# Two transformer blocks on one core: four products that take the high and the low part of their input side by side

## The chip, the core and the metric

The kernel runs on one core of one Trainium2 chip as a single launch. The metric is the device time of a launch in microseconds (us). Before the change three runs gave 1110.01, 1111.19 and 1111.45 us; their median is 1111.19 us. The engines are called PE (matrix products), PEld (loading the stationary operand of a product), DVE (vector engine), ACT (scalar engine), POOL and SP. Each engine works through its own list of instructions in the order in which the program issues them, and waits for others by semaphores.

## What is computed

Two transformer blocks over 256 tokens of width 1024, in float32. The products that the change touches lie in the first block:

```
u = rms_norm(h, norm_mix)
z, xbc, dt_raw, q_a, c_kv, k_rope, gate_ssd, gate_mla = split_cols(u @ w_in, ...)
xbc = silu(causal_depthwise_conv(xbc, conv_w, conv_b))      # 4 taps along the tokens
xs, bm, cm = split_cols(xbc, (2048, 512, 512))
...                                                         # state space scan, 4 groups of 8 heads
y = y * silu(z)
...
q = rms_norm(h, norm_xattn) @ w_xq                          # attention over 256 memory rows
k, v = split(rms_norm(mem, norm_mem) @ w_xkv)
```

The four outputs that are made in another way are x (2048 columns of `w_in`), z (2048), the memory keys k (1024) and the cross queries q (1024). The B and C columns of `w_in`, the gates and the memory values stay as they are, and so do the experts of the first block and all of the second block.

## The kernel before, in words

**Precision.** An operand a is kept as a high part ah, its value rounded to the type that PE multiplies at full speed (fp32r), and a low part al = a - ah. A product is ah·bh + ah·bl + al·bh, three matmuls that add up in one PSUM tile (`mm3`, L263 to L265). The input u has its two parts in the tiles `uh` and `ul` (128 partitions, 8 blocks of 128 features, 256 tokens).

**Weights.** They come in units of 128x1024 numbers. A transfer on SP's queue fills `raw`; ACT rounds it to `whi` (L237); DVE makes `wlo = raw - whi` (L238). `run` issues these splits up to three units (`LP`) ahead of the unit that PE multiplies, and each ring of tiles (`raw`, `whi`, `wlo`) has four places, so a split also waits until PE is done with the unit four back.

**The products with features on partitions** (`gemm_fm`). A unit holds 4 of the 8 feature blocks for two chunks of 128 output columns. An item is one chunk with one unit: 4 feature blocks, 12 matmuls of 128x128 weights against 256 tokens. Two units, four items, give a pair of chunks, each in the first 256 columns of a PSUM tile of 512 (`acc`, 4 buffers). After a chunk's last matmul its evacuation is issued at once, in the same item:

- x (`ev_x`, `conv`): ACT applies the first tap and the bias to the PSUM tile (L704), then DVE adds three more taps, each reading the PSUM tile again (L707).
- z (`ev_z`, L777), memory keys (`ev_k`, L1122) and cross queries (`ev_q`, L1182): one copy by ACT.

**Order.** `schedule` merges three lists (closing steps, the chain of small steps, the large products) by fixed costs and by latencies in a table; `run` issues the items in that order, with the splits of later units between them. The large products of this stage run as: B and C mixed with z of groups 0 and 1; x of group 0 (from about 78 us); x of group 1 mixed with half of a gate product (91 to 119 us); z of group 2; x of group 2 (138 to 149 us); z and x of group 3 mixed; the other gates. The small steps of a group g, in their order: silu of x and z (`sil`), the product C·B (`cb`, L797 on PE), transposes of x scaled by dt (`xt`, L785, L787), eight decay matrices (`decay`: PE L809 to L813, ACT's exponentials L816, DVE's product M, L817), and four products with them (`ymm`, PE L828, DVE L834 and L836). The decays take turns with the products: four decays, product 0, two decays, product 1, two decays, products 2 and 3. `bcs` is the silu of all of B and C (`bT`, `cT`), after which the first `cb` can run.

The lines that decide how the evacuation of x works before the change:

```
nc.scalar.activation(y, src, AF.Identity, bias=..., scale=...)               # src: the PSUM tile
for j in (2, 1, 0):
    o = 3 - j
    nc.vector.scalar_tensor_tensor(y[:, o:], src[:, :T - o], c[...], y[:, o:], op0=ALU.mult, op1=ALU.add)
```

Of the kernel before, what the change touches and what calls it, by code (L numbers as in the profile page):

```python
# [9 lines left out]
F32 = mybir.dt.float32  # L10
F32R = mybir.dt.float32r
# [7 lines left out]
P = 128  # L19
NT = 2  # L20
T = 256
# [91 lines left out]
class K:  # L113
# [147 lines left out]
    def mm3(self, out, ah, al, bh, bl, start, stop):  # L261
# [2 lines left out]
        mm(out, ah, bl, start=False, stop=False)  # L264
        mm(out, al, bh, start=False, stop=stop)  # L265

    def acc(self):
        return self.pp.tile([P, 512], F32, tag="acc", name=self.nm("acc"), bufs=4)

# [83 lines left out]
            out += a[i:i + n] + b[i:i + n]  # L353
        return out

    def gemm_fm(self, w, c0, nch, kt, xT, evac, name, deps=(), held=None):


        items = []
        hiT, loT = xT  # L360
        for i in range(0, nch, 2):
            st = {}
            for k0 in range(0, kt, 4):
                nk = min(4, kt - k0)
                u = self.unit(w, k0, nk, c0 + i * P, 256)
                for c in range(2):
                    def fn(u=u, k0=k0, c=c, st=st, i=i, nk=nk):
                        if k0 == 0:
                            st[c] = self.chb() if held is not None and i == 4 else self.acc()
                        a = st[c][:, :T]  # L370
                        for kk in range(nk):
                            k = k0 + kk
                            s = slice(c * P, (c + 1) * P)
                            self.mm3(a, u.hi[:, kk, s], u.lo[:, kk, s], hiT[:, k, :], loT[:, k, :],
                                     start=(k == 0), stop=(k == kt - 1))
                        if k0 + 4 >= kt and (held is None or i >= 6):
                            evac(i + c, a)
                    if k0 + 4 >= kt and held is not None and i < 6:
                        held.append(Item(lambda c=c, i=i, st=st: evac(i + c, st[c][:, :T]), name=f"{name}.{i + c}"))
                    items.append(Item(fn, [u], nk * 3 * 0.109, f"{name}.{i + c}" if k0 + 4 >= kt and (held is None or i >= 6) else None))  # L380
        self.set_deps(items, deps)
        return items
# [100 lines left out]
    def phase_a(self):  # L483
# [43 lines left out]
            nc.gpsimd.tensor_copy(self.identb, self.ident)  # L527
            nc.gpsimd.tensor_copy(nmb, self.c[:, C_NEGM:C_NEGM + P])

        uh = pu.tile([P, 8, T], F32R, name="uh", tag="uh")  # L530
        ul = pu.tile([P, 8, T], F32R, name="ul", tag="ul")
        A["u"] = u = (uh, ul)
        chain, main = [], []

        def start_a():
# [162 lines left out]
                  Item(lambda: qnorm(1), cost=1.1, name="qn")]  # L698


        def conv(src, ch, y):

            c = self.cols
            nc.scalar.activation(y, src, AF.Identity, bias=c[:, 96 + ch:97 + ch], scale=c[:, 72 + ch:73 + ch])  # L704
            for j in (2, 1, 0):
                o = 3 - j
                nc.vector.scalar_tensor_tensor(y[:, o:], src[:, :T - o], c[:, 24 * j + ch:24 * j + ch + 1], y[:, o:],  # L707
                                               op0=ALU.mult, op1=ALU.add)
# [47 lines left out]
    def ssd_group(self, g):  # L756
# [9 lines left out]
        def ev_x(i, a):  # L766
            if i == 0:
                st["xT"] = ps.tile([P, 4, T], F32, name=self.nm("xT"), tag="xT", bufs=3)
            A["conv"](a, 4 * g + i, st["xT"][:, i, :])
        xdep = [("cols", 0)] + ([(f"g{g - 3}.fin", 0)] if g >= 3 else [])  # L770
        xg = self.gemm_fm(w_in, 2048 + 512 * g, 4, 8, A["u"], ev_x, f"x{g}", xdep)

        def ev_z(i, a):
            if "zs" not in A:
                A["zs"] = self.sp.tile([P, 2, 4, T], F32, name="zs", tag="big8")
            st["z"] = A["zs"][:, g % 2]
            nc.scalar.copy(st["z"][:, i, :], a)  # L777
        zg = self.gemm_fm(w_in, 512 * g, 4, 8, A["u"], ev_z, f"z{g}", [(f"g{g - 2}.y3", 0)] if g >= 2 else [])
        ch = []

        def xt(t):
# [294 lines left out]
    def tail(self):  # L1076
# [24 lines left out]
        def mem_c(t):  # L1101
            def fn():
                if t == 0:
                    A["m"] = tuple(self.cols8(i).bitcast(F32R) for i in (self.S_MH, self.S_ML))
                self.norm_c(("m", t), *A["m"], t, D)
            return fn

# [11 lines left out]
        def ev_k(c, a):  # L1119
            if c == 0:  # L1120
                A["kx"] = self.cols8(self.S_KX)
            nc.scalar.copy(A["kx"][:, c, :], a)  # L1122

        def ev_v(t, b, a):
            if t == 0 and b == 0:
# [4 lines left out]
        fill += self.gemm_fm(w, 0, 8, 8, self.lazy("m"), ev_k, "kx", [("m1", 2)])  # L1130
        fill += self.gemm_tm(w, 1024, 1024, 2, 8, self.lazy("m"), ev_v, "vx")


# [45 lines left out]
        def ev_q(c, a):  # L1179
            if c == 0:  # L1180
                st["q"], st["xp"] = self.cols8(self.S_MH), self.cols8(self.S_ML)
            nc.scalar.copy(st["q"][:, c, :], a)  # L1182
        qx = self.gemm_fm(I["w_xq"][0], 0, 8, 8, self.lazy("u"), ev_q, "qx", [("nx1", 2), ("vx.1", 0)])
        sc = 1.0 / 16

        def scores(hh, t):
# [1031 lines left out]
        return self.schedule([start, hg, sb, nrm, main])  # L2218


class _Lazy:

    def __init__(self, d, key, i=None):
# [32 lines left out]
```

## Time and profile before

| | |
|---|---|
| median of three runs | 1111.19 us |
| the profiled execution | 1112.61 us, of which its span is 1110.8 us |
| PE busy | 1049.5 us (94%) |
| PEld busy | 895.8 us (81%) |
| DVE busy | 632.7 us (57%) |
| ACT busy | 515.0 us (46%) |
| POOL busy | 142.6 us (13%) |
| mean granted clock of PE | 0.983 of full speed |

The share of busy time is a mean over stages with different limits. PE's matmuls overlap in the record (a matmul is shown for 0.28 us though the next one starts 0.12 us later), so a busy PE is not a PE without gaps; what a matmul costs in a stream is read from the distance between starts.

### The profile page before, as it was taken

Reading aid. Unit: us, or ns where it says so; the run is one execution under the profiler, and the core shown is the slowest. Engines: PE = TensorE matmul, PEld = TensorE weight load, DVE = VectorE, ACT = ScalarE, POOL = GpSimd, SP = SyncE. Lnnn points to the kernel's source line nnn. Section 1 sums busy time; section 2 is a strip of 40 time slices with the busy share of each in tenths; the row PEclk is TensorE's granted clock in tenths of the full one; section 3 lists DMA queues with packets and bytes.
Section 4 is the critical chain, followed back from the end, with each engine's and each line's share of the span. In section 5 each row is a group of like instructions: output and inputs, shape, how many; then the busy total and the mean of one; then the engine's idle time right before and its main releaser. Section 6 shows DMA issues by size and latency. Waiting matters only on the chain. (4 is left out here: it accounts for less than half of the span.)

```text
span 1110.8 us, 18654 instructions
## 1 busy us (share of the span) xinstructions
PE 1049.5 (94%) x7433; PEld 895.8 (81%) x7433; DVE 632.7 (57%) x1070; ACT 515.0 (46%) x900; POOL 142.6 (13%) x187
## 2 busy tenths in 40 slices
PE   6999999999999899999998897997999999999998
PEld 6999888878887698987675553697888799999876
DVE  4887788766766654545211110278865665555445
ACT  4658676645554454532000000166577555454433
POOL 5410221230002100001000000153501100000000
PEclk9999999999999999999999998998999999999999
DMA  7665434464443999569999999853523465556642
GB/s 255 188 191 153 132 115 139 135 181 137 135 144 115 311 348 314 161 219 327 420 413 420 413 418 413 312 177 104 189 73 120 132 219 180 190 174 192 188 149 95
DMA packets 135035, 241.33 MB, mean 217 GB/s; under 512 B 6924, under 2 KB 88336, under 8 KB 127776
## 3 DMA queue, kind: packets, MB, share of 16 engines
q1 hardware_dynamic: 132160, 231.31, 60.6%
q0 software_dynamic: 2496, 7.74, 2.2%
q8 instruction: 60, 0.98, 0.4%
q10 hardware_dynamic: 288, 1.05, 0.3%
q14 instruction: 31, 0.25, 0.1%
HBM read 239.02 MB, written 1.05 MB: 216 GB/s over the span
## 5 line engine op out<-in xcount | busy, mean ns | idle before, releaser
L238 DVE TENSOR_TENSOR wlo<-raw,whi 128x1024 fp32r<-128x1024 f32 (+1 forms) x240 | 293.5, 1235 | 156.8 <-ACT whi L237 156.1
L237 ACT CAST whi<-raw 128x1024 fp32r<-128x1024 f32 (+1 forms) x240 | 247.3, 1042 | 122.5 <-PE acc L265 59.3
L263 PE MATMUL acc<-ew,whi 128*128 128x256 f32 x528 | 150.2, 284 | 1.3 <-ACT whi L237 0.9
L265 PE MATMUL acc<-ew,wlo 128*128 128x256 f32 x528 | 149.8, 284 | 1.5 <-DVE wlo L238 1.5
L264 PE MATMUL acc<-ew,whi 128*128 128x256 f32 x528 | 149.8, 284 | 0.1
L263 PE MATMUL acc<-uh,whi 128*128 128x256 f32 x384 | 111.2, 290 | 0.0
L264 PE MATMUL acc<-ul,whi 128*128 128x256 f32 x384 | 108.6, 283 | 0.0
L265 PE MATMUL acc<-uh,wlo 128*128 128x256 f32 x384 | 108.5, 283 | 0.0
L263 PEld LDWEIGHTS acc<-ew,whi 128*128 128x128 f32 x528 | 100.5, 190 | 2.0 <-ACT whi L237 1.3
L265 PEld LDWEIGHTS acc<-ew,wlo 128*128 128x128 f32 x528 | 100.2, 190 | 2.1 <-DVE wlo L238 2.1
L264 PEld LDWEIGHTS acc<-ew,whi 128*128 128x128 f32 x528 | 100.3, 190 | 0.6 <-DVE ew L1753 0.6
L263 PEld LDWEIGHTS acc<-uh,whi 128*128 128x128 f32 x384 | 73.5, 191 | 0.8 <-issue 0.3
L264 PEld LDWEIGHTS acc<-ul,whi 128*128 128x128 f32 x384 | 73.6, 192 | 0.2
L265 PEld LDWEIGHTS acc<-uh,wlo 128*128 128x128 f32 x384 | 73.5, 191 | 0.0
L1556 PE MATMUL acc<-ew,xe 128*32 128x256 f32 x688 | 59.1, 406 | 9.0 <-DMA ew<-in_w_exp_gate_dram 5.1
L263 PE MATMUL acc<-whi,uh 128*128 128x512 f32 (+1 forms) x160 | 62.6, 391 | 0.5 <-ACT whi L237 0.5
L1515 PEld LDWEIGHTS acc<-Gr,h 128*128 128x128 f32 x256 | 54.5, 299 | 10.6 <-issue 9.6
L264 PE MATMUL acc<-wlo,uh 128*128 128x512 f32 (+1 forms) x160 | 61.3, 383 | 1.8 <-DVE wlo L238 1.8
L265 PE MATMUL acc<-whi,ul 128*128 128x512 f32 (+1 forms) x160 | 61.0, 381 | 0.4 <-DVE ul L422 0.4
L1515 PE MATMUL acc<-Gr,h 128*128 128x128 f32 x256 | 54.6, 373 | 5.8 <-DVE Gr L1496 5.8
L1556 PEld LDWEIGHTS acc<-ew,xe 128*32 128x32 f32 x688 | 35.0, 116 | 27.8 <-DMA ew<-in_w_exp_gate_dram 6.5
L263 PE MATMUL acc<-whi,ew 128*128 128x512 f32 x112 | 45.2, 404 | 1.2 <-ACT ew L421 1.2
(558 smaller groups left out, 2173.1 us busy)
## 6 DMA issues: line engine op xcount, KB each, us to landing
raw<-in_w_in_dram SPq DMA_DIRECT2D x84, 512.0 KB, 4.3
ew<-in_w_exp_down_dram SPq DMA_DIRECT2D x23, 1024.0 KB, 17.0
raw<-in_w_gate_up_dram SPq DMA_DIRECT2D x44, 512.0 KB, 3.8
ew<-in_w_exp_gate_dram SPq DMA_DIRECT2D x17, 1024.0 KB, 16.2
ew<-in_w_exp_up_dram SPq DMA_DIRECT2D x16, 1024.0 KB, 16.6
raw<-in_w_down_dram SPq DMA_DIRECT2D x22, 512.0 KB, 4.2
raw<-in_w_ssd_out_dram SPq DMA_DIRECT2D x16, 512.0 KB, 4.6
raw<-in_w_xkv_dram SPq DMA_DIRECT2D x16, 512.0 KB, 6.3
```

The source lines that it names most:

```text
L237: self.nc.scalar.copy(hi[:, :m], u.raw[:, :m])
L238: self.nc.vector.tensor_sub(lo[:, :m], u.raw[:, :m], hi[:, :m].bitcast(F32))
L263: mm(out, ah, bh, start=start, stop=False)
L264: mm(out, ah, bl, start=False, stop=False)
L265: mm(out, al, bh, start=False, stop=stop)
L1515: nc.tensor.matmul(p[:, j * P:(j + 1) * P], x, st["Gr"][:, t, :], start=(part is None and t == 0), stop=(t == 1 and (part is None or j == 3)))
L1556: nc.tensor.matmul(a[j][CAP * i:CAP * i + CAP, :256], xe[:, k, i * CAP:i * CAP + CAP], w, start=(k == 0), stop=(k == 7))
```

## The change

The two parts of u become one tile `u` with the parts side by side, `[P, 8, 2, T]`; the class `Parts` gives the high part, the low part, or both as one operand of 512 columns. The memory rows get the same layout in the two tiles that they had. For x, z, memory keys and cross queries `mm_wide` takes the place of `mm3`: one matmul of the weights' high part against both parts (512 columns, filling the whole PSUM tile), and one of the weights' low part against the high part (256 columns, added to the first half). The chunk then stands in two halves that must be added: `halves` copies the second half to SBUF with ACT and adds the first half with DVE. For x the sum goes to a new SBUF tile `cx` (2 buffers), and the four taps read that tile.

```diff
+    def mm_wide(self, out, ah, al, b, k, last):
+        mm = self.nc.tensor.matmul
+        bw = b.both(k)
+
+        def wide():
+            mm(out, ah, bw, start=(k == 0), stop=(k == last))
+
+        def narrow():
+            mm(out[:, :T], al, b.hi[:, k, :], start=False, stop=False)
+        for f in (narrow, wide) if k == last else (wide, narrow):
+            f()
+
+    def halves(self, out, a):
+        self.nc.scalar.copy(out, a[:, T:])
+        self.nc.vector.tensor_add(out, a[:, :T], out)
...
-                        a = st[c][:, :T]
+                        a = st[c][:, :T] if wide is None else st[c]
...
+                            if wide is not None:
+                                self.mm_wide(a, u.hi[:, kk, s], u.lo[:, kk, s], wide(), k, kt - 1)
+                                continue
...
-        uh = pu.tile([P, 8, T], F32R, name="uh", tag="uh")
-        ul = pu.tile([P, 8, T], F32R, name="ul", tag="ul")
-        A["u"] = u = (uh, ul)
+        A["uw"] = Parts([pu.tile([P, 8, 2, T], F32R, name="u", tag="u")])
+        A["u"] = u = uh, ul = A["uw"].hi, A["uw"].lo
...
-        def conv(src, ch, y):
+        def conv(src, ch, y, wide=False):
             c = self.cols
+            if wide:
+                x = ps.tile([P, T], F32, name=self.nm("cx"), tag="cx", bufs=2)
+                self.halves(x, src)
+                src = x
             nc.scalar.activation(y, src, AF.Identity, bias=c[:, 96 + ch:97 + ch], scale=c[:, 72 + ch:73 + ch])
...
-            A["conv"](a, 4 * g + i, st["xT"][:, i, :])
+            A["conv"](a, 4 * g + i, st["xT"][:, i, :], True)
...
-            nc.scalar.copy(st["z"][:, i, :], a)
+            self.halves(st["z"][:, i, :], a)
...
-            nc.scalar.copy(A["kx"][:, c, :], a)
+            self.halves(A["kx"][:, c, :], a)
...
-            nc.scalar.copy(st["q"][:, c, :], a)
+            self.halves(st["q"][:, c, :], a)
```

The order of the items does not change, since their costs and latencies do not. In the whole program PE issues 384 matmuls fewer, DVE 48 additions more and ACT 16 copies more (for z, keys and queries the copy was there before). At two places this is what stands on an engine.

ACT, at the first pair of chunks of x in group 1 (`acc` are the two chunks' PSUM tiles, `xT` the result, `cb` the next small step, `whi` a unit's split), before:

```order
L237 CAST whi_1209<-raw_1046 128x1024 [waits DMAHW5_49,PE_49]
L704 ACTIVATE xT_1227<-acc_1181,cols 128x256 [waits PE_49]
L704 ACTIVATE xT_1227<-acc_1194,cols 128x256 [waits PE_49]
L800 COPY cb_1251<-ch_1248 128x384 [waits PE_49]
L237 CAST whi_1253<-raw_1085 128x1024 [waits DMAHW6_49]
L816 ACT_TABLE_LOAD
```

and now:

```order
L237 CAST whi_1124<-raw_981 128x1024 [waits DMAHW5_49,PE_49]
L282 COPY cx_1139<-acc_1104 128x256 [waits PE_49]
L729 ACTIVATE xT_1138<-cx_1139,cols 128x256 [waits DVE_49]
L282 COPY cx_1154<-acc_1113 128x256 [waits PE_49]
L729 ACTIVATE xT_1138<-cx_1154,cols 128x256 [waits DVE_49]
L826 COPY cb_1164<-ch_1161 128x384 [waits PE_49]
L237 CAST whi_1166<-raw_1018 128x1024 [waits DMAHW6_49]
L842 ACT_TABLE_LOAD
```

Between the copy of a chunk and its first tap ACT now waits for DVE, and the second chunk's copy, the next split and the decays' exponentials stand behind that wait.

DVE, at the same pair, before:

```order
L238 TENSOR_TENSOR wlo_1210<-raw_1046,whi_1209 128x1024 [waits DMAHW5_49,PE_49,Activation_49]
L707 SCALAR_TENSOR_TENSOR xT_1227<-acc_1181,cols,xT_1227 128x255 [waits Activation_49]
L707 SCALAR_TENSOR_TENSOR xT_1227<-acc_1181,cols,xT_1227 128x254 [waits DVE_49]
L707 SCALAR_TENSOR_TENSOR xT_1227<-acc_1181,cols,xT_1227 128x253 [waits DVE_49]
L707 SCALAR_TENSOR_TENSOR xT_1227<-acc_1194,cols,xT_1227 128x255 [waits Activation_49]
```

and now:

```order
L238 TENSOR_TENSOR wlo_1125<-raw_981,whi_1124 128x1024 [waits DMAHW5_49,PE_49,Activation_49]
L283 TENSOR_TENSOR cx_1139<-acc_1104,cx_1139 128x256 [waits Activation_49]
L732 SCALAR_TENSOR_TENSOR xT_1138<-cx_1139,cols,xT_1138 128x255 [waits Activation_49]
L732 SCALAR_TENSOR_TENSOR xT_1138<-cx_1139,cols,xT_1138 128x254 [waits DVE_49]
L732 SCALAR_TENSOR_TENSOR xT_1138<-cx_1139,cols,xT_1138 128x253 [waits DVE_49]
L283 TENSOR_TENSOR cx_1154<-acc_1113,cx_1154 128x256 [waits Activation_49]
L732 SCALAR_TENSOR_TENSOR xT_1138<-cx_1154,cols,xT_1138 128x255 [waits Activation_49]
```

Each chunk has one addition more on DVE, and after it the next instruction of DVE waits for ACT, which itself waited for that addition.

## Rows read from the trace of the kernel before

**Rows 1.** Busy times by window: us, engines (x instructions), PEclk, DMA share, GB/s

```profile
100.00:125.00 25.00, 23.92 (x181) 19.74 (x180) 22.66 (x37) 20.09 (x42) 4.08 (x6) 1.00 0.52 160
...
225.00:250.00 25.00, 22.97 (x132) 19.31 (x129) 16.00 (x27) 11.15 (x23) 10.48 (x13) 0.93 0.59 175
```

**Rows 2.** Timeline of PE in two streams: start us, duration us, then the instruction

```profile
95.95 0.28 PE L263 MATMUL acc<-uh,whi 128*128 128x256 f32 x1
...
96.91 0.28 PE L265 MATMUL acc<-uh,wlo 128*128 128x256 f32 x1
...
226.81 0.39 PE L263 MATMUL acc<-whi,uh 128*128 128x512 f32 x1
...
227.95 0.39 PE L265 MATMUL acc<-whi,ul 128*128 128x512 f32 x1
```

**Rows 3.** Groups by shape: count, busy us, mean ns, idle before and its releasers

```profile
L777 ACT COPY zs<-acc 128x256 f32<-128x256 f32 x16 | 5.9, 381 | 9.1 <-PE acc L265 9.0
...
L1223 DVE TENSOR_TENSOR ul<-ch,uh 128x256 fp32r<-128x256 f32 x8 | 3.4, 425 | 3.0 <-ACT uh L1222 3.0
...
L704 ACT ACTIVATE xT<-acc,cols 128x256 f32<-128x256 f32 x16 | 9.0, 575 | 5.8 <-PE acc L265 5.7
...
L707 DVE SCALAR_TENSOR_TENSOR xT<-acc,cols,xT 128x254 f32<-128x254 f32 x16 | 7.7, 482 | 0.6
...
L435 DVE SCALAR_TENSOR_TENSOR qy<-sm,rpow,grow 128x256 f32<-128x256 f32 x2 | 1.0, 478 | 0.0
```

**Rows 4.** Timeline of DVE, groups 0 and 1: in brackets idle before, its releaser

```profile
88.47 1.23 DVE L238 TENSOR_TENSOR wlo<-raw,whi 128x1024 fp32r<-128x1024 f32 x1 [0.55 <-ACT whi L237]
89.61 2.94 DVE L707 SCALAR_TENSOR_TENSOR xT<-acc,cols,xT 128x255 f32<-128x255 f32 x6
...
103.38 1.22 DVE L238 TENSOR_TENSOR wlo<-raw,whi 128x1024 fp32r<-128x1024 f32 x1
...
114.73 1.22 DVE L238 TENSOR_TENSOR wlo<-raw,whi 128x1024 fp32r<-128x1024 f32 x1
...
120.47 1.78 DVE L817 TENSOR_TENSOR M<-M,cb 128x384 f32<-128x384 f32 x2 [0.33 <-ACT M L816]
```

**Rows 5.** Timeline of ACT, 90 to 100 us

```profile
90.39 0.57 ACT L704 ACTIVATE xT<-acc,cols 128x256 f32<-128x256 f32 x1 [0.87 <-PE acc L265]
...
94.53 1.04 ACT L719 ACTIVATE cT<-cT 128x1024 f32<-128x1024 f32 x1
...
99.26 1.01 ACT L704 ACTIVATE xT<-acc,cols 128x256 f32<-128x256 f32 x2
```

**Rows 6.** Timeline of PE, 97 to 123 us

```profile
97.03 0.59 PE L797 MATMUL ch<-cT,bT 128*128 128x256 f32 x2
...
108.49 0.28 PE L265 MATMUL acc<-uh,wlo 128*128 128x256 f32 x1
...
121.40 0.62 PE L828 MATMUL ch<-M,xd 128*64 128x256 f32 x2 [0.79 <-DVE M L817]
122.30 0.86 PE L828 MATMUL ch<-M,xd 128*64 128x256 f32 x6 [0.29 <-DVE M L817]
```

**Rows 7.** Timeline of DVE, last pair of x in group 2

```profile
147.53 1.23 DVE L238 TENSOR_TENSOR wlo<-raw,whi 128x1024 fp32r<-128x1024 f32 x1 [0.50 <-ACT whi L237]
148.67 2.94 DVE L707 SCALAR_TENSOR_TENSOR xT<-acc,cols,xT 128x255 f32<-128x255 f32 x6
151.52 1.02 DVE L817 TENSOR_TENSOR M<-M,cb 128x384 f32<-128x384 f32 x2
```

**Rows 8.** Timeline of PE just behind that pair

```profile
152.22 1.24 PE L828 MATMUL ch<-M,xd 128*64 128x256 f32 x8 [0.74 <-DVE M L817]
```

**Rows 9.** Timeline of PE, a wait and the matmuls of 512 columns behind it

```profile
229.71 0.61 PE L848 MATMUL ch<-consts,ssq 128*128 128x1 f32 x4 [1.38 <-POOL ssq L842]
...
230.52 0.63 PE L264 MATMUL acc<-wlo,uh 128*128 128x512 f32 x1
...
233.51 0.56 PE L265 MATMUL acc<-whi,ul 128*128 128x512 f32 x1
```

More of the change, by code (lines that the diff above doesn't have):

```diff
@@ L354, in mix, with gemm_fm @@
         return out
-    def gemm_fm(self, w, c0, nch, kt, xT, evac, name, deps=(), held=None):
+    def gemm_fm(self, w, c0, nch, kt, xT, evac, name, deps=(), held=None, wide=None):
         items = []
@@ L768, in ev_x @@
                 st["xT"] = ps.tile([P, 4, T], F32, name=self.nm("xT"), tag="xT", bufs=3)
-            A["conv"](a, 4 * g + i, st["xT"][:, i, :])
+            A["conv"](a, 4 * g + i, st["xT"][:, i, :], True)
         xdep = [("cols", 0)] + ([(f"g{g - 3}.fin", 0)] if g >= 3 else [])
-        xg = self.gemm_fm(w_in, 2048 + 512 * g, 4, 8, A["u"], ev_x, f"x{g}", xdep)
+        xg = self.gemm_fm(w_in, 2048 + 512 * g, 4, 8, A["u"], ev_x, f"x{g}", xdep, wide=lambda: A["uw"])
         def ev_z(i, a):
@@ L776, in ev_z @@
             st["z"] = A["zs"][:, g % 2]
-            nc.scalar.copy(st["z"][:, i, :], a)
-        zg = self.gemm_fm(w_in, 512 * g, 4, 8, A["u"], ev_z, f"z{g}", [(f"g{g - 2}.y3", 0)] if g >= 2 else [])
+            self.halves(st["z"][:, i, :], a)
+        zg = self.gemm_fm(w_in, 512 * g, 4, 8, A["u"], ev_z, f"z{g}", [(f"g{g - 2}.y3", 0)] if g >= 2 else [],
+                          wide=lambda: A["uw"])
         ch = []
@@ L1103, in fn @@
                 if t == 0:
-                    A["m"] = tuple(self.cols8(i).bitcast(F32R) for i in (self.S_MH, self.S_ML))
+                    A["mw"] = Parts([self.flat(i).rearrange("p (k a s) -> p k a s", k=4, a=2).bitcast(F32R)
+                                     for i in (self.S_MH, self.S_ML)])
+                    A["m"] = A["mw"].hi, A["mw"].lo
                 self.norm_c(("m", t), *A["m"], t, D)
@@ L1129, in tail @@
         mem = [Item(mem_c(0), cost=1.7, name="m0", deps=[("pt", 0)]), Item(mem_c(1), cost=1.7, name="m1")]
-        fill += self.gemm_fm(w, 0, 8, 8, self.lazy("m"), ev_k, "kx", [("m1", 2)])
+        fill += self.gemm_fm(w, 0, 8, 8, self.lazy("m"), ev_k, "kx", [("m1", 2)], wide=lambda: A["mw"])
         fill += self.gemm_tm(w, 1024, 1024, 2, 8, self.lazy("m"), ev_v, "vx")
@@ L1181, in ev_q @@
                 st["q"], st["xp"] = self.cols8(self.S_MH), self.cols8(self.S_ML)
-            nc.scalar.copy(st["q"][:, c, :], a)
-        qx = self.gemm_fm(I["w_xq"][0], 0, 8, 8, self.lazy("u"), ev_q, "qx", [("nx1", 2), ("vx.1", 0)])
+            self.halves(st["q"][:, c, :], a)
+        qx = self.gemm_fm(I["w_xq"][0], 0, 8, 8, self.lazy("u"), ev_q, "qx", [("nx1", 2), ("vx.1", 0)], wide=lambda: A["uw"])
         sc = 1.0 / 16
@@ L2218, in phase_c, with __init__, __getitem__, both @@
         return self.schedule([start, hg, sb, nrm, main])
+class Parts:
+    class Part:
+        def __init__(self, tiles, i):
+            self.tiles, self.i = tiles, i
+        def __getitem__(self, idx):
+            p, k, s = idx
+            n = self.tiles[0].shape[1]
+            if isinstance(k, slice):
+                t, k = k.start // n, slice(k.start % n, k.start % n + k.stop - k.start)
+            else:
+                t, k = divmod(k, n)
+            return self.tiles[t][p, k, self.i, s]
+    def __init__(self, tiles):
+        self.tiles, self.hi, self.lo = tiles, Parts.Part(tiles, 0), Parts.Part(tiles, 1)
+    def both(self, k):
+        n = self.tiles[0].shape[1]
+        return self.tiles[k // n][:, k % n].rearrange("p a s -> p (a s)")
 class _Lazy:
```

## The prediction

> **What bounds the kernel now.** I read the table of busy times by window first. Between 100 and 125 us PE is busy for 23.92 of 25 us, but DVE for 22.66 and ACT for 20.09 [rows 1]: in the stage where x is made, DVE is nearly as full as PE. So the question is not only what PE saves, but whether DVE and ACT can carry what they are given.
>
> Next, the timeline of PE for the price of a matmul in a stream. Nine matmuls of 256 columns start from 95.95 to 96.91, eight steps of 0.120 us; six of 512 columns from 226.81 to 227.95, five steps of 0.228 [rows 2]. Twice the columns cost less than twice the time; a pair of 256 costs 0.240, so one of 512 instead saves 0.012 us.
>
> Last, the timelines of the three engines in groups 0 and 1, to see who waits for whom. Two kinds of work differ in their lead. The low part of a weight unit is early: the one that DVE starts at 103.38 (1.22 us, so it ends at 104.60) is first read by PE at 108.49 [rows 4, 6], 3.9 us later. The decay matrices M are not: at the end of group 0 PE waits for DVE at 121.40 and 122.30 [rows 6], and the last M, which ends at 120.47 + 1.78 = 122.25 [rows 4], is read 0.05 us later. At the end of group 1 it is the same: PE waits 0.74 us for an M at 152.22 [rows 8], and that M stands on DVE right behind the six taps of the last pair of x [rows 7]. At these two places DVE sets the end, and a delay of DVE goes to PE in full.
>
> **PE: what the change removes.** A step over one block of features goes from 3 x 0.120 to 0.228 + 0.120, 0.012 us less. There are 16 chunks of x, 16 of z, 8 of keys, 8 of queries, 8 steps each: 384 steps, 384 matmuls fewer, 4.6 us if PE never waits. The columns stay the same, 768 a step. [...]
>
> **z, keys and queries.** ACT's copy stays (0.381 us), now of the second half. DVE gets one addition per chunk, of a PSUM and an SBUF operand of 128x256; the nearest row is the subtraction of that shape, 0.425 us [rows 3]. 32 of them are 13.6 us of DVE. Two per pair (0.85 us) fit in the lead of the weight units, 3.9 us where DVE is fullest, so I cost them at nothing. If that cover were gone, the 16 of z alone would cost 6.8 us. No transfer is added; those of the weights follow their splits, as before.
>
> **x: where it costs.** Before, a chunk took ACT one activation from PSUM (0.575 us [rows 3]) and DVE three taps; six taps, two chunks, take 2.94 us [rows 4], 1.47 a chunk. Now it is a chain that crosses twice: ACT's copy (0.381), DVE's addition (0.425), ACT's activation, DVE's three taps (3 x 0.482 [rows 3]). DVE has nothing else to do between its addition and its taps, since its list is in order, and ACT nothing between copy and activation. A hand-over I set at 0.05 us, the step from the M that ends at 122.25 to PE's 122.30. The activation now reads SBUF, which no row shows for it. Its lower bound is the plain copy, 0.381, its upper one its own row, 0.575; I take 0.575, since the operation with its column of scales and of biases is the same. So DVE is taken for 0.425 + 0.05 + 0.575 + 0.05 + 1.45 = 2.55 us a chunk, against 1.47: **1.08 us more per chunk**, 4.3 per group of four. ACT is held for at least 1.48 us a chunk, against 0.575, and longer when DVE comes late to the addition; the second chunk's copy and the next splits queue behind it.
>
> That the taps read SBUF instead of PSUM I cost at no gain: a tap of 254 columns from PSUM takes 482 ns, an operation of the same kind with all of its operands of 256 columns in SBUF 478 [rows 3]. [...]
>
> **The first place, groups 0 and 1 of x (84 to 123 us).** Through group 0's four chunks DVE falls back by 4.3, less 0.8 that PE's chunks come earlier (64 steps of z before it x 0.012), less the wait of 0.55 before 88.47 [rows 4] that is swallowed: 3.0. ACT's list is full from 90.39 on, so the silu of C, which starts at 94.53 and ends at 95.57 [rows 5], ends near 98.5, while PE wants it at 97.03 [rows 6]: PE waits there already. ACT reaches the first pair of group 1 not at 99.26 [rows 5] but near 102. Group 1's chunks add another 4.3: DVE would be 7.3 late behind the second pair, at the row of 114.73. Before the last M two waits go: 0.33 in the row at 120.47, and 0.76 by which that row's two M (1.78) are longer than two that run without waiting (1.02 [rows 4, 7]). 7.3 - 1.1 = 6.2, and PE, which reads that M, is late by all of it. PE's saving so far is spent as waiting.
>
> **The second place, group 2 of x (140 to 158 us).** 4.3 more through four chunks, less the wait of 0.50 before 147.53 [rows 7]: 3.8, again right ahead of the M for which PE waits. The saving in z and x of group 2 is lost too.
>
> **The rest.** In group 3 the large products stand between the taps and the M, and for keys and queries the unit's lead covers the additions: there PE keeps its saving, 64 + 64 + 64 = 192 steps, -2.3 us.
>
> **The sum:** 6.2 + 3.8 - 2.3 = +7.7 us. The profiled execution took 1112.61 us and would take 1120.3; it lies 1.4 above the median of the runs, 1111.2, from which I get **1118.9 us**. With the activation at 0.381 it is 12 x 0.19 = 2.3 less, 1116.6; with the addition at a tap's 0.482 it is 0.7 more, 1119.6.
>
> **The rivals.**
>
> *The lead absorbs it (faster).* If DVE and ACT catch up in the waits of the neighbouring stretches before any M or silu is read, PE never sees the delay and all 384 steps count: -4.6, 1106.6. The 3.9 us of lead of the units speak for it; the 0.05 us of lead of the last M, at both places, against. It decides where the DVE time added between the last idle stretch and the M stays under that lead. Chance 0.10.
>
> *DVE pays for the additions only (same).* If DVE's wait for the activation falls into time in which it waited anyway, a chunk costs 0.425 more, not 1.08: 8 x 0.425 - 0.55 - 1.1 - 0.8 = 1.0 at the first place, 4 x 0.425 - 0.5 = 1.2 at the second, -2.3: 1111.1. Against it stands that in the first place DVE hardly waits at all (22.66 of 25 us). Chance 0.15.
>
> *The clock falls as well (slower still).* [...] Chance 0.15.
>
> **How the numbers follow.** The forecast has the other 0.60. The range, 1109.0 to 1123.0, takes in its bounds, the clock and the "same" case, and leaves out the faster one and little beyond. 0.2% is 2.2 us, about what a measurement of this kernel can tell from no change: faster by more 0.10, within 0.15, slower by more 0.75 (0.60 + 0.15).
>
> **What would show it.** Right: 384 matmuls fewer; the wide ones at 0.228 us a step; DVE idle for about 0.65 us before the first tap of each chunk of x, released by ACT; ACT waiting for DVE in the activation; PE waiting several us in all for M between 119 and 130 us and again behind group 2, and for the silu of C. Wrong: PE's waits at these places as short as now, or the first tap starting right behind the addition. If the wide matmuls took 0.240 us a step, the saving would be nil and only the cost would be left.

## The result and the profile after

The changed kernel takes 1129.69 us (median of five runs, 1128.26 to 1130.94), against 1111.17 for the kernel before: 1.0169 times the time, interval 1.0154 to 1.0184, 18.5 us more. The forecast was 1118.9, in a range of 1109.0 to 1123.0: the sign was right, but the forecast loss of 7.7 us is less than half of what came. The profiled execution took 1129.80 us, with a span of 1127.7.

The head of the page:

```profile
PE 1056.4 (94%) x7049; PEld 881.0 (78%) x7049; DVE 648.6 (58%) x1118; ACT 520.0 (46%) x916; POOL 145.0 (13%) x187
```

384 matmuls fewer, and DVE and ACT with only 15.9 and 5.0 us more work in the whole launch than in the table before the change. So the time has gone into waits, and into PE at half clock (a granted clock of 0.50 in the stretches shown below; before, it was 1.00 from 84 to 229.71 us). Busy times by window (the columns of [rows 1]):

```profile
100.00:125.00 25.00, 22.51 (x122) 18.43 (x123) 16.90 (x27) 16.77 (x31) 0.00 (x0) 0.87 0.42 127
150.00:175.00 25.00, 20.48 (x130) 15.41 (x129) 20.10 (x37) 16.21 (x36) 4.87 (x7) 0.86 0.34 105
200.00:225.00 25.00, 22.28 (x119) 17.84 (x118) 18.77 (x31) 16.16 (x30) 7.08 (x7) 0.86 0.42 121
```

In the window from 100 to 125 us DVE was busy for 22.66 us before [rows 1] and is now for 16.90; ACT went from 20.09 to 16.77. They do less in that time, since each stands waiting; and in all three windows PE's granted clock is 0.86 or 0.87. The waits of PE between 84 and 225 us (line, what it waited for, total us, times, longest):

```profile
PE ch L835 <- ACT M L842: 3.7, 1, 3.7
PE ch L874 <- POOL ssq L868: 2.7, 1, 2.7
PE ch L854 <- DVE M L843: 2.6, 3, 1.6
PE ch L823 <- ACT cT L744: 2.6, 1, 2.6
PE ch L835 <- ACT cb L826: 2.5, 1, 2.5
```

Three of the five are for ACT, 8.8 us; for DVE it is 2.6 us, and it was 2.5 us in five waits before ([rows 6, 8] show three of them). So PE waits for DVE no longer than it did; the waits that came are for ACT, and one for POOL. Where this delays PE is seen at four of its instructions; between the second and the third stands the longest wait, for ACT's exponentials (timeline of PE):

```profile
99.98 1.22 PE L823 MATMUL ch<-cT,bT 128*128 128x256 f32 x2 [2.60 <-ACT cT L744]
...
132.53 0.86 PE L854 MATMUL ch<-M,xd 128*64 128x256 f32 x6 [0.24 <-DVE M L843]
...
164.52 0.22 PE L835 MATMUL ch<-negb,identb 128*128 128x128 bf16 x1 [3.68 <-ACT M L842]
...
165.86 1.92 PE L854 MATMUL ch<-M,xd 128*64 128x256 f32 x8 [0.79 <-DVE M L843]
...
249.31 0.61 PE L874 MATMUL ch<-consts,ssq 128*128 128x1 f32 x4 [1.38 <-POOL ssq L868]
```

The four (at 99.98, 132.53, 165.86 and 249.31) started at 97.03, 122.30, 152.22 and 229.71 before [rows 6, 8, 9]. The delay is 2.95 us at the first product C·B, 10.2 behind the last M of group 0, 13.6 behind x of group 2, 19.6 behind group 3; the rest of the launch takes some of it back. The last step, 6.0 us, is nearly all of it group 3's, for which the forecast had no cost: the C·B of group 3 starts at 208.94 us, and started at 195.01 before, 13.9 us earlier.

The evacuation of x, by groups of one shape (count, busy us, mean ns, idle just before and its releaser):

```profile
L729 ACT ACTIVATE xT<-cx,cols 128x256 f32<-128x256 f32 x16 | 9.6, 601 | 26.6 <-DVE cx L283 26.6
L732 DVE SCALAR_TENSOR_TENSOR xT<-cx,cols,xT 128x255 f32<-128x255 f32 x16 | 7.7, 484 | 10.7 <-ACT xT L729 10.7
L283 DVE TENSOR_TENSOR cx<-acc,cx 128x256 f32<-128x256 f32 x16 | 6.7, 418 | 0.0
L282 ACT COPY cx<-acc 128x256 f32<-128x256 f32 x16 | 5.9, 367 | 0.9 <-PE acc L273 0.9
```

For one chunk DVE is taken for 0.418 + 10.7/16 + 3 x 0.483 = 2.54 us; the forecast had 2.55. ACT is held for 0.367 + 26.6/16 + 0.601 = 2.63 us, where one activation of 0.575 stood before [rows 3]. What that does is seen on ACT ahead of the first C·B (its timeline):

```profile
92.70 0.35 ACT L282 COPY cx<-acc 128x256 f32<-128x256 f32 x1
94.72 0.60 ACT L729 ACTIVATE xT<-cx,cols 128x256 f32<-128x256 f32 x1 [1.67 <-DVE cx L283]
...
98.89 1.04 ACT L744 ACTIVATE cT<-cT 128x1024 f32<-128x1024 f32 x1
99.84 1.03 ACT L237 CAST whi<-raw 128x1024 fp32r<-128x1024 f32 x1
```

The silu of C, at 94.53 before [rows 5], starts at 98.89, 4.36 us later, behind the chunks of group 0, and PE waits 2.60 us for it. The next two splits stand behind that silu on ACT, and DVE waits for them (timeline of DVE, after the change and before):

```profile
100.90 1.23 DVE L238 TENSOR_TENSOR wlo<-raw,whi 128x1024 fp32r<-128x1024 f32 x1 [2.42 <-ACT whi L237]
103.74 1.23 DVE L238 TENSOR_TENSOR wlo<-raw,whi 128x1024 fp32r<-128x1024 f32 x1 [1.62 <-ACT whi L237]
```

```profile
96.54 1.23 DVE L238 TENSOR_TENSOR wlo<-raw,whi 128x1024 fp32r<-128x1024 f32 x1 [2.40 <-ACT whi L237]
99.38 1.23 DVE L238 TENSOR_TENSOR wlo<-raw,whi 128x1024 fp32r<-128x1024 f32 x1 [1.62 <-ACT whi L237]
```

DVE stood still for just as long before. So ACT sets the time of these splits, before as after, and the first moves by the same 4.36 us as the silu. ACT is late since it waited for DVE's additions, PE is late since it waits for ACT, and the next chunks of x come later from PE. Behind the waits the clock falls. The first case is the wait of 2.60 us: the two matmuls at 99.98 are shown for 1.22 us, at a granted clock of 0.50 from 99.98 to 101.20, and for 0.59 before [rows 6], at 1.00. The next one is clearer, PE's products of 512 columns behind the wait of 2.49 us for `cb` (timeline of PE):

```profile
108.87 0.22 PE L835 MATMUL ch<-negb,identb 128*128 128x128 bf16 x1 [2.49 <-ACT cb L826]
...
110.16 0.63 PE L264 MATMUL acc<-wlo,u 128*128 128x512 f32 x1
...
113.14 0.57 PE L265 MATMUL acc<-whi,u 128*128 128x512 f32 x1
113.55 0.40 PE L273 MATMUL acc<-u,whi 128*128 128x512 f32 x1
113.78 0.28 PE L276 MATMUL acc<-u,wlo 128*128 128x256 f32 x1
113.90 0.40 PE L273 MATMUL acc<-u,whi 128*128 128x512 f32 x1
...
116.02 0.40 PE L273 MATMUL acc<-u,whi 128*128 128x512 f32 x1
```

Seven steps from 110.16 to 113.14 are 0.426 us each, at a granted clock of 0.50, against 0.228 [rows 2], at 1.00: 1.4 us. The last four rows give the gain: seven steps of a wide and a narrow matmul from 113.55 to 116.02, 0.353 us each. Three narrow ones took 0.360, so a step saves 0.007 us and not 0.012.

In group 3 the addition of a chunk is late on DVE, and with it ACT, then POOL and PE (timelines of ACT, and of PE up to 222 us):

```profile
201.08 0.41 ACT L282 COPY cx<-acc 128x256 f32<-128x256 f32 x1
204.99 0.60 ACT L729 ACTIVATE xT<-cx,cols 128x256 f32<-128x256 f32 x1 [3.50 <-DVE cx L283]
```

```profile
216.53 1.01 PE L874 MATMUL ch<-consts,ssq 128*128 128x1 f32 x4 [2.72 <-POOL ssq L868]
...
219.49 0.63 PE L264 MATMUL acc<-wlo,u 128*128 128x512 f32 x1
...
222.05 0.63 PE L264 MATMUL acc<-wlo,u 128*128 128x512 f32 x1
```

ACT stands for 3.50 us between the copy and the first tap, PE for 2.72; then six steps of 512 columns, from 219.49 to 222.05, take 0.427 us each: half clock once more (granted 0.50).

Waits and clock together give the whole delay of 19.6 us. From 84 us up to the instruction behind group 3 the waits of PE are 15.5 us (14.1 in the list and 1.38 at 249.31), against 3.9 before (2.5 and the 1.38 of [rows 9]): 11.6 more. The three windows stand for 25 x (0.13 + 0.14 + 0.14) = 10 us of full clock that PE was not granted (an estimate); before, the windows from 75 to 225 us had 1.00. It bounds what the clock costs there from above, since some of it falls into waits. Waits and clock, less the 1.9 us by which the products alone bring PE forward to that place (e3 below), make about 20 us. So the half clock behind the waits may cost nearly as much as the waits.

### The profile page after: what moved, and what is told of

The parts are those of the page before. It is cut to its first block, busy times and chain, and to the rows that moved or that the text cites. A ratio compares the mean times of both kernels' runs of the same rounds, so it can differ in the third digit from the quotient of the medians.

```text
span 1127.7 us, 17951 instructions
## 1 busy us (share of the span) xinstructions
PE 1056.4 (94%) x7049; PEld 881.0 (78%) x7049; DVE 648.6 (58%) x1118; ACT 520.0 (46%) x916; POOL 145.0 (13%) x187
## 5 line engine op out<-in xcount | busy, mean ns | idle before, releaser
L263 PE MATMUL acc<-ew,whi 128*128 128x256 f32 x464 | 131.5, 283 | 0.8 <-ACT whi L237 0.5
L265 PE MATMUL acc<-ew,wlo 128*128 128x256 f32 x464 | 131.2, 283 | 1.0 <-DVE wlo L238 1.0
L264 PE MATMUL acc<-ew,whi 128*128 128x256 f32 x464 | 131.3, 283 | 0.8 <-DVE ew L444 0.7
L273 PE MATMUL acc<-u,whi 128*128 128x512 f32 x320 | 114.9, 404 | 0.0
L264 PEld LDWEIGHTS acc<-ew,whi 128*128 128x128 f32 x464 | 87.7, 189 | 1.4 <-DVE ew L444 0.8
L263 PEld LDWEIGHTS acc<-ew,whi 128*128 128x128 f32 x464 | 87.7, 189 | 1.2 <-ACT whi L237 0.7
L276 PE MATMUL acc<-u,wlo 128*128 128x256 f32 x320 | 83.2, 280 | 0.0
L273 PEld LDWEIGHTS acc<-u,whi 128*128 128x128 f32 x320 | 58.6, 189 | 11.0 <-issue 0.3
L264 PE MATMUL acc<-wlo,u 128*128 128x512 f32 (+1 forms) x160 | 63.1, 394 | 1.6 <-DVE wlo L238 1.6
L263 PE MATMUL acc<-whi,u 128*128 128x512 f32 (+1 forms) x160 | 64.3, 402 | 0.0
L276 PEld LDWEIGHTS acc<-u,wlo 128*128 128x128 f32 x320 | 60.4, 189 | 3.3
L265 PE MATMUL acc<-whi,u 128*128 128x512 f32 (+1 forms) x160 | 62.6, 391 | 0.4 <-DVE u L444 0.4
L263 PE MATMUL acc<-whi,ew 128*128 128x512 f32 x112 | 45.2, 404 | 1.2 <-ACT ew L443 1.2
L265 PE MATMUL acc<-whi,ew 128*128 128x512 f32 x112 | 44.4, 396 | 0.3 <-DVE ew L444 0.3
```

Source lines behind the costliest of these rows:

```text
L263: mm(out, ah, bh, start=start, stop=False)
L273: mm(out, ah, bw, start=(k == 0), stop=(k == last))
L276: mm(out[:, :T], al, b.hi[:, k, :], start=False, stop=False)
```

## The experiments

Two theories stood at the start, A and B in the first expectations: the evacuation of x costs the time, or the wide products and the additions wherever they stand. Then, for how the evacuation does it: L, by the time for which DVE is taken, as the forecast had it; H, by ACT's list standing behind its wait; C, by both together. Each kernel was timed against the kernel before on the same chip; ratios are to that kernel, whose medians lay between 1110.93 and 1111.27 us.

| run | median us | ratio, 95% interval |
|---|---|---|
| e1_x_old | 1109.26 | 0.9982, 0.9973 to 0.9992 |
| e2_x_only | 1129.32 | 1.0156, 1.0142 to 1.0170 |
| e3_no_add | 1106.15 | 0.9955, 0.9941 to 0.9969 |
| e4_evac_only | 1127.88 | 1.0143, 1.0125 to 1.0161 |
| e5_dve_tap | 1118.02 | 1.0069, 1.0044 to 1.0094 |
| e6_late_taps | 1114.07 | 1.0023, 1.0011 to 1.0035 |
| e7_dve_load | 1121.60 | 1.0100, 1.0068 to 1.0131 |
| e8_act_load | 1125.74 | 1.0138, 1.0107 to 1.0168 |
| e9_block2 | 1107.62 | 0.9963, 0.9948 to 0.9977 |
| e10_z3_old | 1127.02 | 1.0136, 1.0115 to 1.0156 |
| e11_x3_only | 1111.85 | 1.0001, 0.9983 to 1.0019 |
| e12_both_loads | 1131.77 | 1.0175, 1.0158 to 1.0192 |
| e13_x01_only | 1120.30 | 1.0072, 1.0052 to 1.0092 |
| e14_x2_only | 1112.27 | 1.0011, 1.0002 to 1.0021 |
| e15_x3_again | 1112.78 | 1.0017, 0.9999 to 1.0034 |
| e16_x3_z3old | 1111.39 | 1.0001, 0.9991 to 1.0010 |

**Which part costs: x alone, or the rest alone.** e1 takes the new way out of x (the lines below), e2 out of the three others:

```diff
-            A["conv"](a, 4 * g + i, st["xT"][:, i, :], True)
+            A["conv"](a, 4 * g + i, st["xT"][:, i, :])
-        xg = self.gemm_fm(..., f"x{g}", xdep, wide=lambda: A["uw"])
+        xg = self.gemm_fm(..., f"x{g}", xdep)
```

> x by three products of 256 columns and evacuated as before the change; z, memory keys and cross queries as in the change. 256 matmuls fewer than before the change, 32 additions more on DVE. Theory A (the evacuation of x costs everything, through the hand-over between ACT and DVE): the loss is gone and the gain of 256 steps x 0.012 us is left, 1108.1 us. Theory B (the wide products themselves, or the additions anywhere, cost the time): two thirds of the loss stay, about 1123 us.

> Only x in the new way; z, keys and queries as before the change. Theory A: the whole loss and less gain than in the change, since 256 of the 384 saved matmuls are back: 1129.7 + 3.1 = 1132.8 us if the saved time of z, keys and queries reached the end, 1129.7 if it was spent as waiting. Theory B: a third of the loss, about 1117 us.

Without x in the new way the loss is gone and about 2 us are gained (0.18%, at the edge of what can be told from no change); with x alone it is all there. So it is x, as theory A has it; whether by its products or by its evacuation the next two runs tell. That z, keys and queries cost nothing on PE agrees with the forecast: in e1 PE's only waits for products of this stage are those that it had before (84 to 260 us: 2.5 us for M, 1.4 for POOL, 0.5 for ACT).

**The products alone, and the evacuation alone.** e3 leaves out the second half of each chunk, which is neither copied nor added, and evacuates as before:

```diff
-        self.nc.scalar.copy(out, a[:, T:])
-        self.nc.vector.tensor_add(out, a[:, :T], out)
+        self.nc.scalar.copy(out, a[:, :T])
```

e4 is the kernel before with the new evacuation of x. It has no second half, so it adds each chunk to its own copy, and x comes out doubled:

```diff
+            if wide:
+                x = ps.tile([P, T], F32, name=self.nm("cx"), tag="cx", bufs=2)
+                nc.scalar.copy(x, src)
+                nc.vector.tensor_add(x, src, x)
+                src = x
```

> All four products in the new way, but the second half of each chunk is left out (neither copied nor added), so that every evacuation is the one from before the change. It shows what the products alone are worth. Theory A: 384 x 0.012 = 4.6 us less than before, 1106.6 us. Theory B with costly wide products: 1111 us or more.

> The kernel before the change, with the chain of copy, addition, first tap and taps of the change for x alone; for want of a second half the addition adds the chunk to its copy, so x comes out doubled. Every product is by three matmuls of 256 columns. It shows the evacuation's price without the products. Theory A: the loss of the change plus the gain that it hides, 1129.7 + 1.5 (x) to 1129.7 + 4.6 (all), 1131 to 1134 us. Theory B with costly wide products: near 1111 us.

The products alone gain 4.8 us (1110.93 to 1106.15), the evacuation of x alone costs 17.0. The 4.8 looks like the forecast's 4.6, but is not made as it was worked out: 384 steps x 0.007 are 2.7 us, and in this run's profile the half clock of [rows 9] did not come, whose seven steps cost 1.4 us, though PE's wait was as long there, 1.37 us (busy times by window, clock 1.00 where [rows 1] have 0.93):

```profile
225.00:250.00 25.00, 22.96 (x145) 19.97 (x144) 16.28 (x31) 12.03 (x26) 9.06 (x12) 1.00 0.66 199
```

Against e2, e4 has 1.4 us less, though its products are the slower ones. The two intervals overlap, so this shows only that the gain of x's own products, 128 steps or 0.9 us, can't be seen at the end.

**How the evacuation costs: DVE's time alone, ACT's time alone, both.** These are the kernel before with idle work behind the first tap of each chunk of x, meant to be without any new wait between the two engines. e7 has the first block, e8 the second, e12 both:

```diff
+            if load:
+                x = ps.tile([P, T], F32, name=self.nm("cx"), tag="cx", bufs=2)
+                nc.vector.tensor_add(x, src, y)
+                nc.vector.tensor_add(x, x, x)
+                nc.vector.tensor_add(x[:, :P], x[:, :P], x[:, :P])
```

```diff
+            if load:
+                x = ps.tile([P, T], F32, name=self.nm("cx"), tag="cx", bufs=2)
+                for _ in range(5):
+                    nc.scalar.copy(x, src)
```

> The kernel before the change, with 1.1 us of idle additions a chunk of x on DVE ahead of its three taps (one of 256 columns from PSUM, one of 256 and one of 128 from SBUF), and nothing else: DVE is taken as long as in the change, ACT is held no longer than before. The result is that of the kernel before. Theory L: all of the 17 us, 1128 us; by the prediction's own sum (6.2 + 3.8 us, with 0.8 us more for lack of the earlier products) 1122 us. Theory H: at most 3 us, 1111 to 1114 us. If both engines are needed (theory C: DVE's lateness and ACT's hold feed each other through PE), between these, about 1117 us.

> The kernel before the change, with five idle copies of 128x256 a chunk of x on ACT behind its first tap (5 x 0.37 = 1.8 us, about as long as ACT is held more in the change: 4.4 to 4.9 us a pair against 1.1), and nothing else: DVE has no more work than before. The result is that of the kernel before. Theory L: 1111 to 1112 us. Theory H: all of the 17 us, 1128 us. Theory C: between them, about 1117 us.

> The kernel before the change, with both idle loads at once: 1.1 us of additions on DVE and 1.8 us of copies on ACT a chunk of x, neither waiting for the other more than before. Alone they cost 10.3 and 14.5 us; the evacuation of the change, in which each waits for the other, costs 17. If the delays only add up: 25 us, 1136 us. If the later engine sets the end at each place, so that the larger counts: 15 to 17 us, 1126 to 1128 us, and then the hand-over costs through the time that the engines are held and through nothing else.

DVE's time alone costs 10.3 us (e7), ACT's load 14.5 (e8), both 20.5 (e12). e7 is what it was meant to be, but for one wait of ACT for DVE, 2.6 us in a silu of x: L, which had all of the 17 us there, falls as the sole cause. e8 is not, as DVE waits for the idle copies before its taps (waits of DVE from 80 to 260 us):

```profile
DVE xT L711 <- ACT cx L708: 15.0, 16, 1.7
```

That is 0.94 us a chunk, so e8 holds DVE nearly as long as the change does (in e12 it is 6.8 us, five waits). By its time alone e8 can't tell ACT's part from DVE's, and no run loads ACT without holding DVE. What parts them are the waits. ACT's own list waits for DVE in e8 as it did before (13.2 us in four waits, at one instruction), so its lateness is its own. The waits of PE from 84 to 260 us are of two kinds, in e7 and then in e8:

```profile
PE ch L833 <- DVE M L822: 7.7, 4, 4.6
PE ch L853 <- POOL ssq L847: 2.4, 2, 1.4
```

```profile
PE ch L813 <- ACT M L820: 3.3, 1, 3.3
PE ch L832 <- DVE M L821: 2.5, 3, 1.6
PE ch L813 <- ACT cb L804: 2.4, 1, 2.4
PE ch L801 <- ACT cT L723: 2.1, 1, 2.1
PE ch L852 <- POOL ssq L846: 1.8, 2, 1.4
```

e8's are the waits of the change, nearly row by row: PE waits for ACT 7.8 us more than before, and for DVE 2.5 us, as before. e7's first row is the wait that the forecast had described. That DVE's added time can delay PE by itself is shown by e7; that ACT's can is read from these waits and not from a run by itself. C fell in its numbers (1117 us for each), and both loads together cost less than the sum. By place, as starts of the same four instructions of PE (timelines; us), with PE's waits up to the last of them beyond the 3.9 us of before, and PE's time at half clock from 84 us up to it:

| | first C·B | behind last M, group 0 | behind x, group 2 | behind group 3 | waits more | at half clock |
|---|---|---|---|---|---|---|
| before | 97.03 | 122.30 | 152.22 | 229.71 | 0 | 0 |
| the change | 99.98 | 132.53 | 165.86 | 249.31 | 11.6 | 20.5 |
| e4, evacuation alone | 99.93 | 132.49 | 167.78 | 247.35 | 10.9 | 13.7 |
| e7, DVE load | 96.83 | 125.01 | 160.05 | 239.43 | 6.2 | 10.2 |
| e8, ACT load | 99.14 | 130.01 | 163.48 | 242.22 | 8.2 | 10.2 |
| e12, both loads | 99.45 | 133.20 | 169.86 | 252.16 | 15.8 | 17.1 |

Up to the last M of group 0 e7 delays PE by 2.7 us and e8 by 7.7, of 10.2 in the change: there ACT decides. Between that and x of group 2 it is 5.1 and 3.6, against 3.4 in the change: either is enough, in e7 by the wait of 4.6 us for M, in e8 and the change by that of 3.3 and 3.7 us for ACT. The last stretch, with group 3, costs 1.9 and 1.2 alone, 4.8 with both, 6.0 in the change. In e4, whose products save nothing, the added waits and half of the time at half clock (10.9 + 6.8) make up the delay of 17.6 us; in e7, e8 and e12 they exceed theirs by up to 2 us, as some of the low clock fell into waits.

**Taking the hand-over apart.** e5 gives the first tap to DVE, so that nothing goes back to ACT. e6 keeps every operation, and puts the copy and the addition of the pair's second chunk ahead of both first taps (`cx` has three buffers there instead of two):

```diff
-            nc.scalar.activation(y, src, AF.Identity, bias=..., scale=...)
+                nc.vector.tensor_scalar(y, src, c[...], c[...], op0=ALU.mult, op1=ALU.add)
```

```diff
+            x = ps.tile([P, T], F32, name=self.nm("cx"), tag="cx", bufs=3)
+            self.halves(x, src)
+            if ch % 2 == 0:
+                A["pend"] = (x, ch, y)
+                return
+            pair = (A["pend"], (x, ch, y))
+            for f in (tap0, taps):
+                for t in pair:
+                    f(*t)
```

> The change, with the first tap and the bias of x on DVE, from the sum in SBUF, so that nothing goes back to ACT: ACT is held for one copy a chunk and never waits for DVE there. DVE has the addition (0.42 us), a first tap of 0.25 to 0.48 us and three taps (1.45 us): 2.1 to 2.35 us a chunk, against 2.55 in the change and 1.47 before it. The evacuation alone cost 17 us (evacuation-only run), the products alone gain 4.8 us. Theory L (the cost follows the time for which DVE is taken): 17 x 0.65/1.08 to 17 x 0.88/1.08 is 10 to 14 us, less 4.8: 1116 to 1120 us. Theory H (the cost is ACT's list standing behind its wait for DVE): 0 to 2 us of cost are left, 1106 to 1109 us.

> The change, with the evacuation of x reordered: the first chunk of a pair is copied and added when it is ready, the second too, and only then come both first taps on ACT and all six taps on DVE. Neither engine should wait for the other for more than 0.2 us; DVE has 0.42 us more a chunk than before the change, ACT 0.37 us more. Theory L: 17 x 0.45/1.08 = 7 us less 4.8: about 1113 us. Theory H: ACT never stands still, 0 to 2 us of cost, 1106 to 1109 us. The rival of the prediction in which DVE pays for the additions only gave 1111 us.

The 0.25 us at the lower end of the first tap was the author's estimate: the shortest operation of that kind and shape in the trace of before takes 0.294 us (L1891). Both came out where L had them (1118.0 and 1114.1), and not as fast as H had. PE's waits in e5, 84 to 260 us:

```profile
PE ch L856 <- DVE M L845: 7.4, 7, 4.0
PE ch L876 <- POOL ssq L870: 3.5, 2, 2.1
```

With ACT free, the waits for it are gone, and DVE's added time alone is left; DVE is busy for 24.24 of 25 us in the window from 100 to 125. With L right here and 6 us too high in e7, what fits all of these runs is that either engine's added time delays PE, where that engine's result is read next. The order of e6 gets back most of the loss (15.6 us faster than the change: 1114.07 against 1129.69, though measured at different times): ACT waits for the additions of x 5.4 us in all, against 26.6 in the change, and PE is at half clock for 3.4 us up to the place behind group 3, against 20.5. Yet even so x in the new way is no gain.

**Place by place.** The change with x in the new way in groups 0 and 1 (e13), in group 2 (e14), in group 3 (e11 and, the same kernel once more, e15), and in group 3 with z of group 3 as before (e16); e10 is the change with only z of group 3 as before. The diff shows the condition of e13, and that for z:

```diff
-            A["conv"](a, 4 * g + i, st["xT"][:, i, :], True)
+            A["conv"](a, 4 * g + i, st["xT"][:, i, :], g < 2)
...
+            self.halves(st["z"][:, i, :], a) if g < 3 else nc.scalar.copy(st["z"][:, i, :], a)
```

> The change, with z of group 3 alone by three products and one copy. In the trace of the change the third place (group 3) costs 5.6 us, in the run with x alone 1.3 us. If the difference is the additions of z, which stand on DVE between those of x: about 4 us less than the change, 1125.5 us. If it is the earlier places' delay carried on: 1129.7 us and a little over.

> The change, with x in the new way in group 3 alone; groups 0 to 2 of x as before. If each place costs by itself: the 1109.3 us of the run with the old x and the third place's 5.6 us, about 1115 us. If the third place costs only because the first two made everything late: 1109 us. By the prediction (group 3 is covered): 1108.5 us.

> The change, with x in the new way in groups 0 and 1 alone. If the places add up: the 1109.3 us of the run with the old x and the 9.7 us that the trace of the change shows up to the last decay matrix of group 0, 1119 us. By the price of the prediction (6.2): 1115.5 us.

> The change, with x in the new way in group 2 alone. If the places add up: 1109.3 and 4.7 us, 1114 us. By the price of the prediction (3.8): 1113.1 us. If group 2 costs only because the engines come to it late: 1109 to 1110 us.

> The kernel with x in the new way in group 3 alone, once more: two sets of times again, near 1108.5 and near 1114 us, if the third place is at an edge; in a profile of the faster kind the wait for POOL's sum of squares (2.7 us in the slower one) and the half clock behind it are missing.

> x in the new way in group 3 alone, and z of group 3 as before the change. If the additions of z between those of x decide the third place: no loss there, 1109 to 1110 us in all runs. If the chain of x does it by itself: about 1114 us, at least in some runs.

At the instruction behind group 3, where e1 stands at 228.74, e13 stands at 240.16, e14 at 233.47, e11 at 234.82 and e15 at 233.17: 11.4, 4.7 and 6.1 or 4.4 us, 20.6 to 22.2 in all, and the change is 20.6 behind e1. So the places cost by themselves and add up there. In the totals they add up less: 11.0, 3.0 and 2.6 to 3.5 us over e1's median. Behind that instruction e14 and e15 get time back: there they are 3.8 and 3.5 us behind the kernel before, and yet their spans are shorter than its own, 1110.0 and 1109.5 against 1110.8 us. e1, 1.0 us ahead there, ends 1.9 ahead (1108.9). What takes the delay back wasn't found.

At that instruction group 3's delay comes mostly with the new way for z: with it e11 and e15 are 6.1 and 4.4 us behind e1, without it (e16, 230.55) 1.8. The totals do not show it: e16's median, 1111.39 us, is not the 1109 to 1110 that was expected, and can't be told from e11's and e15's. In the change itself their removal (e10) gave 2.7 us (1127.02), not the 4 that was expected. The set of two times that e11 seemed to show did not come back as such: e15's ten runs spread over 1107.96 to 1116.38, and its profile has the same wait of 2.7 us for POOL as that of e11, though it took 1111.30 us. The spread goes with the granted clock, as a mean over the launch: e11's five shortest runs (up to 1108.88 us) have 0.984 to 0.987, its seven longer ones (from 1111.06 us) 0.978 to 0.982; e15's two shortest 0.987, its others 0.977 to 0.982. In the profiles the window from 200 to 225 us has 0.86 in e11 and 0.93 in e15, so behind that same wait e11 is at half clock for twice as long, which is the 1.7 us between them at that place. What decides, behind equal waits, whether and for how long the clock falls stays open.

**Where the engines have room.** e9 is e1 with the gate and up products of the second block in the new way as well:

```diff
+            x = pt([P, T], "fw", bufs=2)
+            self.halves(x, a)
-            nc.scalar.activation(g, a, AF.Silu)
+            nc.scalar.activation(g, x, AF.Silu)
...
+            self.gemm_fm(wgu, ..., wide=lambda: self.A["u2w"])
```

> x as before the change; z, keys and queries in the new way, and also the gate and up products of the second block (44 chunks, 352 steps): copy by ACT, addition by DVE, then the activation or the product from SBUF. Around those products DVE is busy for 14 of 25 us and ACT for 12, and nothing of theirs is read soon after. If the products' gain is kept where both engines have room: the 1109.3 us of the run with the old x, less 352 x 0.012 = 4.2, 1105 us. If the hand-over costs by itself wherever it stands: 1109 us or more.

1107.62 us, 0.37% faster than before and the fastest complete version. DVE and ACT take the additions without PE standing still for them, with time left (busy times by window):

```profile
910.00:935.00 25.00, 25.00 (x144) 21.85 (x143) 17.61 (x26) 13.89 (x26) 0.00 (x0) 1.00 0.57 178
```

The gain over e1, 1.6 us, is less than the 4.2 expected: a step of three takes 0.358 there (medians 0.119, 0.120 and 0.119 us from start to start) and one of two 0.353 (0.233 and 0.120), so 352 steps are worth 1.8 us. The same overestimate as in the forecast.

## Why the prediction was right or wrong

**Right.** The sign, and that DVE and ACT and not PE would decide. The chain on DVE: 2.54 us a chunk against 2.55, its wait of 0.67 us for ACT against 0.65. z, keys and queries are covered for PE (but see group 3). The taps read SBUF at 0.482 to 0.484 us, as from PSUM [rows 3]: costing this at no gain was right.

**Right by luck.** The second place is 3.4 us against 3.8, but the forecast had it as a wait for DVE's M. PE waited 0.79 us for that M, as before (0.74), and 3.68 us for ACT's exponentials, which stood behind the four chunks of x on ACT. The waits in all, 11.6 us more against the 10.0 of the forecast's two places, are near for the same reason: another engine's waits. And e7, DVE's time alone, came to 1121.6 us, where the forecast's sum gave 1122, but not at its places: 2.7 us at the first for 7.0, 5.1 for 3.8, 1.9 for none.

**Wrong, the first step: "DVE sets the end, and a delay of DVE goes to PE in full"; ACT's hold had no term in the sum.** The forecast saw that ACT is "held for at least 1.48 us a chunk" and that the silu of C would be late, and then took the last M's delay, 6.2 us, for the whole of the first place, as if PE's earlier waits lay inside it. Measured are 2.63 us a chunk for ACT and 10.2 us. PE waited for ACT 8.8 us up to 225 us, and for M 2.6, as before: by the forecast's own sign of being wrong, waits for M "as short as now". The silu was 4.36 us late, not 3.0, and PE, being late for it and for `cb`, is late with the next chunks.

The 6.2 us were not DVE's price either. They carry the 3.0 us of group 0 on into group 1, but in the trace of before DVE waits 2.40 and 1.62 us for the splits between the two groups. e7 shows what happens to them (timeline of DVE):

```profile
97.69 1.22 DVE L238 TENSOR_TENSOR wlo<-raw,whi 128x1024 fp32r<-128x1024 f32 x1
99.26 1.23 DVE L238 TENSOR_TENSOR wlo<-raw,whi 128x1024 fp32r<-128x1024 f32 x1 [0.35 <-ACT whi L237]
```

The waits shrink to none and 0.35 us, the second split starts where it did before (99.38), and what is left for the last M is group 1's part: 2.7 us.

**Wrong, the second step: "In group 3 the large products stand between the taps and the M".** They do, but z's additions, the last decays and the products of group 2 and the splits stand between x's chunks on DVE, so that ACT, having copied a chunk, waited 3.50 us for its addition, and PE behind it 2.72 us for POOL's sum of squares, which follows DVE's results. 6.0 us in the place of a gain of 0.8.

**Wrong, the third step: the chance of the clock.** It had 0.15. Waits of up to 0.79 us [rows 6] had not lowered it (1.00 in the windows of before from 75 to 225 us). But the forecast itself made waits of 6 and 4 us, and behind the one of 1.38 us in [rows 9] seven steps of 512 columns, from 230.52 to 233.51, are 0.427 us each, at a granted clock of 0.50 (busy times by window, before):

```profile
230.50:233.51 3.01, 3.01 (x8) 2.31 (x7) 1.03 (x4) 0.00 (x0) 2.91 (x5) 0.50 0.46 148
```

It belonged in the main case. No run shows what the range allows for the clock (its upper end is 4.1 us over the forecast); the change showed three windows at 0.86 or 0.87, up to 10 us. By size this is the largest term that the sum lacks. The two counts of waits and clock fit the delay, but no run has the waits without the half clock, and a wait as long as that of [rows 9] was not always followed by it (e3).

**Too large, the gain.** The wide matmul's 0.228 us was read in a stream of 512 columns only; beside narrow ones a pair takes 0.353. 2.7 us for 384 steps, not 4.6. The forecast took 12 ns a matmul, the step shows 7.

The range was too narrow for the same reason as the sum: its upper end added the clock to a DVE term alone. That the rivals "lead absorbs" and "additions only" did not come was foreseen rightly; e6, where DVE waits 2.0 us in all for the first taps instead of 10.7, is the nearest to the second, and even it lost 2.8 us.

## What to carry to other kernels

A step that crosses from one in-order engine to another and back took time from both here (2.54 us of DVE a chunk against 1.47, 2.63 of ACT against 0.575): cost it on each engine's list separately, with the wait included, and follow for each list what PE reads next from it, before adding anything up. Look also for the engine's waits between the two places: in e7 the delay of group 0 ended in two waits of DVE, 2.40 and 1.62 us before, none and 0.35 there. Saving matmuls by work on the engines that evacuate paid where these had room: the same exchange gained 1.6 us in the second block and lost some 20 in the stage that makes x. If a forecast contains a PE wait as long as one behind which the trace shows half clock (1.38 us in [rows 9]), the clock belongs in the forecast and not among its rivals: here it may have cost nearly as much as the waits.

## What was not expected of the hardware

A wide and a narrow matmul in turn take 0.353 us, more than the 0.348 of 0.228 + 0.120 from streams of one kind. The activation with a column of scales takes 601 ns from SBUF, 575 from PSUM [rows 3]: no gain for ACT from SBUF, but a small loss.
